# Moving the residual halves of stationary weights by 64 bytes, and what makes room for it, in a single-precision decoder block

## The chip, the cores and the metric

The kernel runs on one core of a Trainium2 chip. The metric is the device time of one execution in microseconds (us); three runs gave a median of 1689.5 us.

## The reference, cut to what matters

One layer of a decoder block on 256 tokens with a model width of 2048, all in single precision:

```python
proj = x @ w_in                              # 2048 -> 13336 columns: q, k, v, gates of both mixers
y_gla = gated_linear_attention(...) @ w_branch_gla
y_fox = forgetting_attention(...) @ w_branch_fox
x = layer_norm(ALPHA * x + (sigmoid(ma) * y_gla + sigmoid(mb) * y_fox) @ w_out)
g = causal_dwconv(x @ w_gate, conv_w, conv_b)          # width 3 over the tokens, 5632 channels
x = layer_norm(ALPHA * x + (gelu(g) * (x @ w_up)) @ w_down)
x = x + sigmoid(x @ w_ple_gate) * (p @ w_ple_proj)
```

Nearly all the work is products of 256 tokens with weight matrices that are each read once.

## The kernel before, in words

**Split products.** A single-precision operand v is split into hi, which is v rounded to the format that TensorE takes at full rate (fp32r), and lo = v - hi. A product of two operands is three of such halves: hi by hi, lo by hi and hi by lo. ScalarE writes hi (`copy`, the activations of L96) and VectorE writes lo (the subtractions, L163 for most of the weights).

**Units.** The weights come in 284 units of 128 x 2048 elements, numbered u in the order of their use. `prep` (L150) takes one unit in two halves, for each of which SyncE loads a `raw` tile of 128 x 1024, ScalarE makes `hi` and VectorE makes `lo`. `unit` (L169) hands the next one out and keeps two more prepared ahead. `prep_s` (L128) with `pair512` (L116) does it for those units of the down projection that go by a seven-product scheme.

**Two ways of using a unit.** TensorE holds one operand, the stationary one, of 128 x 128, and streams the other, the moving one, past it; each product has its own weight load (PEld in the profile), which runs beside the product ahead of it.

- Weights stationary: `w_unit` (L221). For each of 16 slices of the contraction, hi is the stationary operand and streams 512 columns, the tokens' hi and lo side by side (L227). Then lo is stationary and streams the 256 columns of the tokens' hi (L229). The two are called a pair here. The stages, by the names of their results: psfq, psfk, psq, psk (u 0 to 31), psm (u 64 to 95), psa and psb (u 96 to 119), psg and psu (gate and up, u 136 to 223). The first three units of gate and up go through `w_phase` (L233), which streams 256 columns at a time.
- Activations stationary: `x_half` with `x_mm` (L285, L258, products at L271). The tokens' hi or lo is stationary and 512 columns of the weights' hi or lo stream past. The stages are gv and gr (u 32 to 63), wo (u 120 to 135), pg (last 16 units). The down projection dn (L1101, u 224 on) has activations stationary as well.

In psfq to psk, psm, gv and gr small products of the attention are put between the large ones (`pull`); psa, psb, psg and psu have none between them.

**Where the tiles lie.** The pools are laid out one after another. Numbers are bytes within a partition. The six places of hi start at 25,088 and follow each other every 4,096, and those of lo start at 49,664, every 4,096: all are multiples of 512. `gap` (L64) puts unused columns ahead of rhi (96 columns) and behind rlo (192 columns). The work tiles `s8`, which hold activations, lie at 75,008 and every 8,192 after it: each starts 256 bytes past a multiple of 512. So in `w_unit` the moving operand starts 256 past a multiple of 512 and the stationary one at a multiple; in `x_half` it is the other way round.

**First stage.** fv takes 16 half units of 128 x 1048 of its own (`fv_prep`, L338), with activations stationary and three moving chunks of 352, 352 and 344 columns (`fch`, L335; products at L381). The hi and lo tiles are `s8` tiles with their first column at the tile's start. Both halves of the first unit are loaded in three chunks each, the others whole. Two of the five `raw` places are taken at first by `held` tiles, which GpSimd releases by a copy that waits for a lo tile (L361 for the first half of unit 0, L364 for its second half): the loads of later halves, which need these places, wait for that on SyncE's queue.

**Gate.** In the loop over 44 blocks (L1017) the gate's result is combined into `gp`, one of two tiles of 264 columns whose first two columns are zero for good (L991). GpSimd copies two columns behind the data (L1023), and VectorE takes the three taps of the convolution from it (L1025, L1030).

**Work tiles t1 and t2** are rings of six places each, of 256 and 512 columns, for short-lived results.

Of the kernel before, what the change touches and what calls it, by code (L numbers as in the profile page):

```python
# [9 lines left out]
F32 = mybir.dt.float32  # L10
F32R = mybir.dt.float32r
# [8 lines left out]
P = 128  # L20
# [6 lines left out]
FH = 8  # L27
# [5 lines left out]
NS = 1048  # L33


GAPS = (96, 192, 64)
P_STAT = 5000
P_LN1 = (4000, 2000)
P_LN2 = (4000, 1000)
# [17 lines left out]
def tile_block(ctx: ExitStack, tc: tile.TileContext, wu, wfv, wpp, xT_in, x_in, pT_in, wlr,  # L57
               chan, gnorm, lng, ident_in, mask_in, cmask_in, out):
    nc = tc.nc
# [20 lines left out]
    def s8(shape, dt=F32, name=None):  # L80
        return big.tile(shape, dt, tag="S8", name=name)
# [4 lines left out]
    def t2(name):  # L86
        return sm.tile([P, 512], F32, tag="t2", bufs=6, name=name)
# [7 lines left out]
    def copy(o, i, scale=1.0):  # L95
        return nc.scalar.activation(o, i, AF.Copy, bias=0.0, scale=scale)  # L96
# [16 lines left out]
            for i, n in enumerate(DN_ORDER[nh]) if n in DN_S}  # L113
    ready = {}

    def pair512(a, b, name):  # L116

        hi, lo = [r.tile([P, 1024], F32R, tag=t, name=f"{t}{name}")
                  for r, t in ((rhi, "hi"), (rlo, "lo"))]
        out = []  # L120
        for src, e in ((a, slice(0, 512)), (b, slice(512, 1024))):
            if src is not None:
                copy(hi[:, e], src)
                nc.vector.tensor_tensor(lo[:, e], src, hi[:, e].bitcast(F32), ALU.subtract)
                out.append((hi[:, e], lo[:, e]))
        return out

    def prep_s(u):  # L128

        r0, r1 = [ring.tile([P, 1024], F32, tag="raw", bufs=5, name=f"raw{u}_{h}")  # L130
                  for h in range(2)]
        for h, r in enumerate((r0, r1)):
            nc.sync.dma_start(r, wu[u, :, h * 1024:(h + 1) * 1024])
        b12, b11, b22, b21 = r0[:, 0:512], r0[:, 512:1024], r1[:, 0:512], r1[:, 512:1024]
        ops = pair512(b11, None, f"b11_{u}")
        hi = rhi.tile([P, 1024], F32R, tag="hi", name=f"hi{u}_1")
        copy(hi, r1)
        lo = rlo.tile([P, 1024], F32R, tag="lo", name=f"lo{u}_1")
        nc.vector.tensor_tensor(lo, r1, hi.bitcast(F32), ALU.subtract)
        ops += [(hi[:, 512:1024], lo[:, 512:1024]), (hi[:, 0:512], lo[:, 0:512])]  # L140
        ts = {}
        for n, a, b in (("T1", b12, b11), ("T3", b12, b22), ("T2", b22, "T1"),
                        ("T4", b21, "T2")):
            ts[n] = t2(f"{n}_{u}")
            nc.vector.tensor_tensor(ts[n], a, ts.get(b, b) if isinstance(b, str) else b,
                                    ALU.subtract)
        ops += pair512(ts["T1"], ts["T3"], f"t13_{u}") + pair512(ts["T2"], ts["T4"], f"t24_{u}")
        ready[u] = ops

    def prep():  # L150
        u = n_prep[0]
        n_prep[0] += 1
        if u in dn_s:
            prep_s(u)
            return
        his, los = [], []
        for h in range(2):
            raw = ring.tile([P, 1024], F32, tag="raw", bufs=5, name=f"raw{u}_{h}")
            nc.sync.dma_start(raw, wu[u, :, h * 1024:(h + 1) * 1024])
            hi = rhi.tile([P, 1024], F32R, tag="hi", name=f"hi{u}_{h}")  # L160
            copy(hi, raw)
            lo = rlo.tile([P, 1024], F32R, tag="lo", name=f"lo{u}_{h}")
            nc.vector.tensor_tensor(lo, raw, hi.bitcast(F32), ALU.subtract)  # L163
            his.append(hi)
            los.append(lo)
        ready[u] = (his, los)
# [165 lines left out]


    fv = s8([P, 2, 1024], name="fv")
    fch = ((0, 352), (352, 352), (704, 344))  # L335
    fbk = [[mmtile(f"fv_{t}{c}") for c in range(3)] for t in range(2)]

    def fv_prep(u, hs=(0, 1), his=None, los=None):  # L338
        his, los = his or [], los or []
        for h in hs:  # L340
            raw = ring.tile([P, NS], F32, tag="raw", bufs=5, name=f"fvraw{u}_{h}")
            hi = s8([P, NS], F32R, name=f"fvhi{u}_{h}")
            lo = s8([P, NS], F32R, name=f"fvlo{u}_{h}")
            if u > 0:
                nc.sync.dma_start(raw, wfv[u, :, h, :])
            for o, n in fch if u < 2 else ((0, NS),):
                e = slice(o, o + n)
                if u == 0:
                    nc.sync.dma_start(raw[:, e], wfv[u, :, h, e])
                copy(hi[:, e], raw[:, e])  # L350
                nc.vector.tensor_tensor(lo[:, e], raw[:, e], hi[:, e].bitcast(F32), ALU.subtract)
            his.append(hi)
            los.append(lo)
        return his, los
# [3 lines left out]
    held = [ring.tile([P, NS], F32, tag="raw", bufs=5, name=f"held{i}") for i in range(2)]  # L358
    load_x(0, 0, 1, 1)
    f0 = fv_prep(0, (0,))  # L360
    nc.gpsimd.tensor_copy(held[0][:, 0:1], f0[1][0][:, NS - 1:NS].bitcast(F32))  # L361
    load_x(0, 1, 2, 1)
    fvu = [fv_prep(0, (1,), *f0)]
    nc.gpsimd.tensor_copy(held[1][:, 0:1], f0[1][1][:, NS - 1:NS].bitcast(F32))  # L364
    load_x(0, 2, 4)
    fvu.append(fv_prep(1))
    for u in range(8):
        hi, lo = fvu[u]
        for j in range(2):
            kt = 2 * u + j  # L370
            a = xT[kt // 4][:, kt % 4, :]
# [6 lines left out]
            for t, i, c in seq:  # L378
                o, n = fch[c]
# [27 lines left out]
    for t in range(2):  # L407
        tk = t1("smtok")
        nc.gpsimd.memset(tk, 0.0)
        for i in range(3):  # L410
            copy(tk[:, 32 * i:32 * i + 16], fbk[t][2][:, 320:336])
        copy(tk[:, P:P + FH], fbk[t][2][:, 336:344])
        nc.tensor.transpose(smp[:GROWS, t * P:t * P + P], tk[:, 0:GROWS], ident)
        nc.tensor.transpose(smp[:FH, 256 + t * P:256 + t * P + P], tk[:, P:P + FH], ident)
    for t in range(2):
        for c, (o, n) in enumerate(fch):
            n = min(n, 1024 - o)
# [145 lines left out]
    for nm, dst, sc in (("fq", fq, P ** -0.5), ("fk", fk, 1.0)):  # L563
        if nm == "fk":
            mixers.append(fox_gen())
        for n in range(8):
            hi, lo = unit()
# [415 lines left out]


    tc.keep_in_program_order(nc.scalar.preload_act_table_set("gelu_apprx_tanh_and_others"))


    gp = [late.tile([P, 264], F32, name=f"gp{i}") for i in range(2)]
    late.tile([P, GAPS[2]], F32, name="gap2")
    for i in range(2):  # L990
        nc.gpsimd.memset(gp[i][:, 0:2], 0.0)  # L991
    hC, hS, hY, yps = {}, {}, [], {}

    def sums(y, pair):
# [21 lines left out]

    for n in range(NF):  # L1017
        psg = gate_up(f"psg{n}")
        g = gp[n % 2]
        comb(psg, g[:, 2:258])  # L1020
        cw = [chn[:, c_cw + j * NF + n:c_cw + j * NF + n + 1] for j in range(3)]
        for i in range(2):
            nc.gpsimd.tensor_copy(g[:, 258 + i:259 + i], g[:, 129 - i:130 - i])  # L1023
        y = t1("yc")
        nc.vector.tensor_scalar(y, g[:, 2:258], cw[2], chn[:, c_cb + n:c_cb + n + 1],  # L1025
                                ALU.mult, ALU.add)
        y3 = y.rearrange("p (b n) -> p b n", b=2)
        for j, o in ((1, 1), (0, 0)):
            tap = g[:, o:o + 264 - 4 * o].rearrange("p (b n) -> p b n", b=2)[:, :, 0:P]
            nc.vector.scalar_tensor_tensor(y3, tap, cw[j], y3, ALU.mult, ALU.add)  # L1030
        nc.scalar.activation(y, y, AF.Gelu_apprx_tanh, bias=0.0, scale=1.0)
        psu = gate_up(f"psu{n}")
        u = t1("up")
        comb(psu, u)
        pair, j = n // 2, n % 2
        if pair in DN_S:
            if j == 0:
                if pair in DN_Y:
                    if not hY:
                        hY.append(s8([P, len(DN_Y), 2, 256], name="hY"))  # L1040
                    yps[pair] = hY[0][:, DN_Y.index(pair)]
                else:
# [310 lines left out]
```

## Time and profile before

| | |
|---|---|
| three runs | 1688.66, 1689.5, 1692.32 us |
| profiled execution | 1692.31 us, of which the span 1690.2 us |
| TensorE products, weight loads | busy 1679.6 us and 1445.2 us |
| VectorE, ScalarE | busy 1178.1 us and 861.7 us |
| GpSimd | busy 37.4 us |
| granted clock of TensorE | 1.000 |

The span runs from the first to the last instruction; the 2.1 us between it and the execution's own time lie around it. A row of a group of instructions has the line, the engine, the operation, result<-operands with buffer numbers left out, the count, then the busy time in us and the mean ns of one, and last the engine's idle time ahead of them with what ended it. The end of a product in the trace is modelled, and a product's time reaches into that of the next one: start to start is less than the mean of one.

### The profile page before, as it was taken

How to read it: one execution, taken by the hardware profiler on the slowest of the kernel's cores; microseconds unless marked ns; L12 is line 12 of the kernel's file. 1: busy time of each engine (PE TensorE's matmuls, PEld its weight loads, DVE VectorE, ACT ScalarE, POOL GpSimd, SP SyncE). 2: the span in 40 equal slices, each digit the busy share in tenths (PEclk: the TensorE clock that was granted, in tenths of full speed). 3: DMA queues.
4: the chain of work that ended last, by engine and by line, in shares of the span. 5: the costliest groups of instructions: out<-in, count | busy, mean ns of one | idle time of the engine just before them, and what ended most of it. 6: DMA issues, size and time to landing. Idle time of an engine off the chain costs nothing.

```text
span 1690.2 us, 23985 instructions
## 1 busy us (share of the span) xinstructions
PE 1679.6 (99%) x8986; PEld 1445.2 (86%) x8986; DVE 1178.1 (70%) x1762; ACT 861.7 (51%) x1267; POOL 37.4 (2%) x125
## 2 busy tenths in 40 slices
PE   9999999999999999999999999999999999999998
PEld 8888888888888888888888888888888888887887
DVE  7656658768756547774687777766666798788764
ACT  6645445445555544444364444444444465455543
POOL 0100000000000000000010000000000000000000
PEclk9999999999999999999999999999999999999999
DMA  8755555555555555557655665555555556677544
GB/s 318 254 178 164 169 180 182 176 183 177 177 174 173 162 188 193 191 188 290 215 175 188 211 212 187 187 187 186 186 185 189 188 173 209 205 257 245 177 167 169
DMA packets 91717, 330.24 MB, mean 195 GB/s; under 512 B 10264, under 2 KB 11936, under 8 KB 90448
## 3 DMA queue, kind: packets, MB, share of 16 engines
q1 hardware_dynamic: 90816, 324.51, 57.8%
q0 software_dynamic: 784, 4.20, 0.7%
q8 instruction: 70, 1.15, 0.3%
q14 instruction: 47, 0.39, 0.1%
HBM read 323.42 MB, written 5.25 MB: 194 GB/s over the span
## 4 chain that ended last, share of the span: by engine, by line
PE 89%; DVE 5%; DMA 4%; issue 1%; ACT 0%; SPq 0%; POOL 0%; DVEq 0%; ACTq 0%
PE psu L227 10%; PE psg L227 9%; PE psm L227 7%; PE gr L271 5%; PE gv L271 5%; PE psu L229 5%; PE wo L271 5%; PE pg L271 5%; PE dn L1101 5%; PE psg L229 5%; PE psm L229 4%; PE psa L227 3%; DMA raw<-in_wu_dram 3%; PE fv L381 2%; PE psa L229 2%; PE psk L227 2%
## 5 line engine op out<-in xcount | busy, mean ns | idle before, releaser
L163 DVE TENSOR_TENSOR lo<-raw,hi 128x1024 fp32r<-128x1024 f32 x536 | 653.9, 1223 | 392.0 <-ACT hi L96 391.3
L96 ACT ACTIVATE hi<-raw 128x1024 fp32r<-128x1024 f32 x552 | 583.8, 1060 | 656.0 <-issue 263.9
L227 PE MATMUL psu<-x1T,hi 128*128 128x512 f32 x688 | 245.0, 399 | 0.0
L227 PE MATMUL psg<-x1T,hi 128*128 128x512 f32 x672 | 239.3, 399 | 0.0
L229 PE MATMUL psu<-x1T,lo 128*128 128x256 f32 x688 | 193.2, 281 | 0.0
L229 PE MATMUL psg<-x1T,lo 128*128 128x256 f32 x672 | 188.7, 281 | 0.0
L227 PE MATMUL psm<-xT,hi 128*128 128x512 f32 x512 | 180.1, 395 | 0.0
L227 PEld LDWEIGHTS psu<-x1T,hi 128*128 128x128 f32 x688 | 129.3, 188 | 32.2
L227 PEld LDWEIGHTS psg<-x1T,hi 128*128 128x128 f32 x672 | 126.3, 188 | 31.5
L229 PE MATMUL psm<-xT,lo 128*128 128x256 f32 x512 | 143.4, 280 | 0.0
L229 PEld LDWEIGHTS psu<-x1T,lo 128*128 128x128 f32 x688 | 130.0, 189 | 0.0
L229 PEld LDWEIGHTS psg<-x1T,lo 128*128 128x128 f32 x672 | 127.0, 189 | 0.0
L1101 PE MATMUL dn<-hi,hC 128*128 128x512 f32 x448 | 124.0, 389 | 1.2 <-ACT hi L96 1.2
L227 PEld LDWEIGHTS psm<-xT,hi 128*128 128x128 f32 x512 | 96.0, 187 | 21.8
L1101 PEld LDWEIGHTS dn<-hi,hC 128*128 128x128 f32 x448 | 84.0, 188 | 19.0 <-ACT hi L96 1.6
L229 PEld LDWEIGHTS psm<-xT,lo 128*128 128x128 f32 x512 | 96.7, 189 | 0.2
L227 PE MATMUL psa<-oT,hi 128*128 128x512 f32 x256 | 89.5, 391 | 0.0
L271 PE MATMUL gv<-hi,xT 128*128 128x512 f32 x256 | 72.3, 394 | 0.0
L271 PE MATMUL gr<-hi,xT 128*128 128x512 f32 x256 | 72.2, 394 | 0.0
L229 PE MATMUL psa<-oT,lo 128*128 128x256 f32 x256 | 71.7, 280 | 0.0
L1101 PE MATMUL dn<-lo,hC 128*128 128x512 f32 x224 | 70.6, 390 | 0.7 <-DVE lo L163 0.7
L271 PE MATMUL wo<-hi,mT 128*128 128x512 f32 x256 | 70.2, 390 | 0.0
(285 smaller groups left out, 2768.6 us busy)
## 6 DMA issues: line engine op xcount, KB each, us to landing
raw<-in_wu_dram SPq DMA_DIRECT2D x568, 512.0 KB, 4.0
fvraw<-in_wfv_dram SPq DMA_DIRECT2D x14, 524.0 KB, 6.7
lnb<-in_lng_dram SPq DMA_DIRECT2D x4, 1024.0 KB, 9.6
z<-in_x_dram SPq DMA_DIRECT2D x2, 1024.0 KB, 7.6
praw<-in_wpp_dram SPq DMA_DIRECT2D x4, 512.0 KB, 5.8
x1d<-z POOLq DMA_DIRECT2D x2, 1024.0 KB, 5.9
z<-x1d SPq DMA_DIRECT2D x4, 512.0 KB, 5.8
xraw<-in_xT_dram SPq DMA_DIRECT2D x7, 256.0 KB, 6.8
```

The source lines that it names most:

```text
L96: return nc.scalar.activation(o, i, AF.Copy, bias=0.0, scale=scale)
L163: nc.vector.tensor_tensor(lo, raw, hi.bitcast(F32), ALU.subtract)
L227: nc.tensor.matmul(ps, lhsT=hi[i // 8 if hoff == 0 else 0][:, w0 % 1024:w0 % 1024 + P], rhs=a[:, kt % 4, :], start=first and i == 0, stop= ...
L229: nc.tensor.matmul(ps[:, 256:512], lhsT=lo[i // 8 if hoff == 0 else 0][:, w0 % 1024:w0 % 1024 + P], rhs=a[:, kt % 4, 0:256], start=False, ...
L271: nc.tensor.matmul(bs[j][:, 0:m], lhsT=x, rhs=v[:, o:o + m], start=first and i == 0, stop=last and i == 2)
L381: nc.tensor.matmul(fbk[t][c][:, 0:n], lhsT=x, rhs=w[:, o:o + n], start=kt == 0 and i == 0, stop=kt == 15 and i == 2)
L1101: nc.tensor.matmul(ps, lhsT=x, rhs=w, start=todo[id(ps)] == total[id(ps)], stop=todo[id(ps)] == 1)
```

## The change

Three parts.

**Lo tiles.** The places of lo grow from 1024 to 1152 columns (4,608 bytes, still a multiple of 512). The new `lo_tile` gives back 1024 columns of such a place, from column 16 on (64 bytes) for units whose weights are stationary, and from column 0 for units whose activations are (u 32 to 63, 120 to 135, 224 to 283). hi stays where it was. The gap behind rlo shrinks from 192 to 64 columns, so that the work tiles still start 256 bytes past a multiple of 512.

**Gate.** The two `gp` tiles go. Each block takes a `t2` tile instead, and GpSimd writes its two zero columns anew each time, 44 times in all.

**First stage.** The chunks are 384, 384 and 280 columns. The hi and lo tiles of fv begin 64 columns (256 bytes) into their places, so that each chunk starts at a multiple of 512 bytes. Only the first half of unit 0 is loaded in chunks. The copy that releases the first `held` tile waits for the lo of the second half of unit 0, and the one for the second waits for the lo of the first half of unit 1.

```diff
-GAPS = (96, 192, 64)
+GAPS = (96, 64, 80)
+LO_SHIFT = 16
+UA = (range(32, 64), range(120, 136), range(224, 284))
...
+    def lo_tile(u, name):
+        o = 0 if any(u in r for r in UA) else LO_SHIFT
+        return rlo.tile([P, 1152], F32R, tag="lo", name=f"lo{name}")[:, o:o + 1024]
...
-            lo = rlo.tile([P, 1024], F32R, tag="lo", name=f"lo{u}_{h}")
+            lo = lo_tile(u, f"{u}_{h}")
             nc.vector.tensor_tensor(lo, raw, hi.bitcast(F32), ALU.subtract)
...
-    fch = ((0, 352), (352, 352), (704, 344))
+    fch = ((0, 384), (384, 384), (768, 280))
...
-            hi = s8([P, NS], F32R, name=f"fvhi{u}_{h}")
-            lo = s8([P, NS], F32R, name=f"fvlo{u}_{h}")
-            if u > 0:
+            hi = s8([P, 64 + NS], F32R, name=f"fvhi{u}_{h}")[:, 64:]
+            lo = s8([P, 64 + NS], F32R, name=f"fvlo{u}_{h}")[:, 64:]
+            chunked = u + h == 0
+            if not chunked:
                 nc.sync.dma_start(raw, wfv[u, :, h, :])
...
     f0 = fv_prep(0, (0,))
-    nc.gpsimd.tensor_copy(held[0][:, 0:1], f0[1][0][:, NS - 1:NS].bitcast(F32))
     load_x(0, 1, 2, 1)
     fvu = [fv_prep(0, (1,), *f0)]
-    nc.gpsimd.tensor_copy(held[1][:, 0:1], f0[1][1][:, NS - 1:NS].bitcast(F32))
+    nc.gpsimd.tensor_copy(held[0][:, 0:1], f0[1][1][:, NS - 1:NS].bitcast(F32))
     load_x(0, 2, 4)
-    fvu.append(fv_prep(1))
+    f1 = fv_prep(1, (0,))
+    nc.gpsimd.tensor_copy(held[1][:, 0:1], f1[1][0][:, NS - 1:NS].bitcast(F32))
+    fvu.append(fv_prep(1, (1,), *f1))
...
-    gp = [late.tile([P, 264], F32, name=f"gp{i}") for i in range(2)]
     late.tile([P, GAPS[2]], F32, name="gap2")
-    for i in range(2):
-        nc.gpsimd.memset(gp[i][:, 0:2], 0.0)
...
     for n in range(NF):
         psg = gate_up(f"psg{n}")
-        g = gp[n % 2]
+        g = t2(f"gp{n}")
+        nc.gpsimd.memset(g[:, 0:2], 0.0)
         comb(psg, g[:, 2:258])
```

The order of the large products on TensorE is the same in both programs. The following shows where other queues differ. First, SyncE's queue at the start of the program before (x is the activations, fvraw the halves of the first stage's weights):

```order
L183 DMA xraw<-in_xT_dram 128x256
L349 DMA fvraw_0_136<-in_wfv_dram 128x352 x2
L349 DMA fvraw_0_136<-in_wfv_dram 128x344
L183 DMA xraw<-in_xT_dram 128x256
L349 DMA fvraw_1_153<-in_wfv_dram 128x352 x2
L349 DMA fvraw_1_153<-in_wfv_dram 128x344
L183 DMA xraw<-in_xT_dram 128x512
L345 DMA fvraw_0_170<-in_wfv_dram 128x1048
L345 DMA fvraw_1_180<-in_wfv_dram 128x1048
L345 DMA fvraw_0_226<-in_wfv_dram 128x1048
```

And the same queue after the change:

```order
L191 DMA xraw<-in_xT_dram 128x256
L359 DMA fvraw_0_136<-in_wfv_dram 128x384 x2
L359 DMA fvraw_0_136<-in_wfv_dram 128x280
L191 DMA xraw<-in_xT_dram 128x256
L355 DMA fvraw_1_152<-in_wfv_dram 128x1048
L191 DMA xraw<-in_xT_dram 128x512
L355 DMA fvraw_0_167<-in_wfv_dram 128x1048
L355 DMA fvraw_1_178<-in_wfv_dram 128x1048
L355 DMA fvraw_0_224<-in_wfv_dram 128x1048
```

The second half of unit 0 has become one load; the order is otherwise the same, and the last two rows wait for the `held` places, one half unit later than before. Second, GpSimd's queue in the gate loop before the change, where the x1d transfer writes a layer norm's result out:

```order
L1023 COPY gp_8163<-gp_8163 128x1 x2
L1023 COPY gp_8164<-gp_8164 128x1 x2
L982 DMA x1d<-z_7211 128x2048
L1023 COPY gp_8163<-gp_8163 128x1 x2
L1023 COPY gp_8164<-gp_8164 128x1 x2
```

And after it:

```order
L1028 MEMSET gp_8738 128x2
L1028 MEMSET gp_8850 128x2
L1028 MEMSET gp_8960 128x2
L1032 COPY gp_8518<-gp_8518 128x1 x2
L1032 COPY gp_8628<-gp_8628 128x1 x2
L993 DMA x1d<-z_7209 128x2048
L1032 COPY gp_8738<-gp_8738 128x1 x2
L1032 COPY gp_8850<-gp_8850 128x1 x2
```

The zeroing of a block's tile stands several blocks ahead of its copies, and x1d has kept its place between the copies of the sixth and the seventh block.

More of the change, by code (lines that the diff above doesn't have):

```diff
@@ L114, in tile_block, with pair512 @@
     ready = {}
-    def pair512(a, b, name):
-        hi, lo = [r.tile([P, 1024], F32R, tag=t, name=f"{t}{name}")
-                  for r, t in ((rhi, "hi"), (rlo, "lo"))]
+    def lo_tile(u, name):
+        o = 0 if any(u in r for r in UA) else LO_SHIFT
+        return rlo.tile([P, 1152], F32R, tag="lo", name=f"lo{name}")[:, o:o + 1024]
+    def pair512(u, a, b, name):
+        hi = rhi.tile([P, 1024], F32R, tag="hi", name=f"hi{name}")
+        lo = lo_tile(u, name)
         out = []
@@ L134, in prep_s @@
         b12, b11, b22, b21 = r0[:, 0:512], r0[:, 512:1024], r1[:, 0:512], r1[:, 512:1024]
-        ops = pair512(b11, None, f"b11_{u}")
+        ops = pair512(u, b11, None, f"b11_{u}")
         hi = rhi.tile([P, 1024], F32R, tag="hi", name=f"hi{u}_1")
         copy(hi, r1)
-        lo = rlo.tile([P, 1024], F32R, tag="lo", name=f"lo{u}_1")
+        lo = lo_tile(u, f"{u}_1")
         nc.vector.tensor_tensor(lo, r1, hi.bitcast(F32), ALU.subtract)
@@ L146, in prep_s @@
                                     ALU.subtract)
-        ops += pair512(ts["T1"], ts["T3"], f"t13_{u}") + pair512(ts["T2"], ts["T4"], f"t24_{u}")
+        ops += pair512(u, ts["T1"], ts["T3"], f"t13_{u}") + pair512(u, ts["T2"], ts["T4"], f"t24_{u}")
         ready[u] = ops
@@ L347, in fv_prep @@
                 e = slice(o, o + n)
-                if u == 0:
+                if chunked:
                     nc.sync.dma_start(raw[:, e], wfv[u, :, h, e])
@@ L410, in tile_block @@
         for i in range(3):
-            copy(tk[:, 32 * i:32 * i + 16], fbk[t][2][:, 320:336])
-        copy(tk[:, P:P + FH], fbk[t][2][:, 336:344])
+            copy(tk[:, 32 * i:32 * i + 16], fbk[t][2][:, 256:272])
+        copy(tk[:, P:P + FH], fbk[t][2][:, 272:280])
         nc.tensor.transpose(smp[:GROWS, t * P:t * P + P], tk[:, 0:GROWS], ident)
```

## The prediction

> **What bounds the kernel now.** I read the page first. Its parts on busy time and on the chain say that TensorE is never out of work:
>
> ```profile
> PE 1679.6 (99%) x8986; PEld 1445.2 (86%) x8986; DVE 1178.1 (70%) x1762; ACT 861.7 (51%) x1267; POOL 37.4 (2%) x125
> PE 89%; DVE 5%; DMA 4%; issue 1%; ACT 0%; SPq 0%; POOL 0%; DVEq 0%; ACTq 0%
> ```
>
> Next the view of waits, for TensorE alone, its longest first:
>
> ```profile
> PE fv L381 <- ACT fvhi L96: 1.4, 1, 1.4
> PE warm_ps L106 <- DVE warm L103: 1.2, 1, 1.2
> PE dn L1101 <- ACT hi L96: 1.2, 1, 1.2
> ```
>
> No wait is worth more than 1.4 us. So the change can save much only by making the products follow each other faster, and the question is whether they do so at one rate. The view of windows counts the products in two stretches of 100 us in which nothing but pairs of L227 and L229 runs, psa and psb first, then psg and psu. Its columns are the stretch, its length, busy time (count) of TensorE, weight loads, VectorE, ScalarE and GpSimd, then the clock, the DMA share and GB/s:
>
> ```profile
> 660.00:760.00 100.00, 100.00 (x579) 88.19 (x578) 71.62 (x109) 48.34 (x72) 0.00 (x0) 1.00 0.59 190
> 1000.00:1100.00 100.00, 100.00 (x568) 86.77 (x567) 70.64 (x108) 50.07 (x74) 3.35 (x18) 1.00 0.58 186
> ```
>
> The same instructions, at the same clock and with TensorE busy throughout: 200 / 579 = 0.3454 us for a pair in the first, 200 / 568 = 0.3521 in the second. The difference is 6.7 ns a pair. The timeline shows it product by product, first in psb, then in psu (start and duration in us):
>
> ```profile
> 699.84 0.39 PE L227 MATMUL psb<-ofT,hi 128*128 128x512 f32 x1
> 700.19 0.39 PE L227 MATMUL psb<-ofT,hi 128*128 128x512 f32 x1
> 700.53 0.39 PE L227 MATMUL psb<-ofT,hi 128*128 128x512 f32 x1
> 700.88 0.39 PE L227 MATMUL psb<-ofT,hi 128*128 128x512 f32 x1
> ```
>
> ```profile
> 899.84 0.40 PE L227 MATMUL psu<-x1T,hi 128*128 128x512 f32 x1
> 900.08 0.28 PE L229 MATMUL psu<-x1T,lo 128*128 128x256 f32 x1
> 900.20 0.40 PE L227 MATMUL psu<-x1T,hi 128*128 128x512 f32 x1
> 900.43 0.28 PE L229 MATMUL psu<-x1T,lo 128*128 128x256 f32 x1
> 900.55 0.40 PE L227 MATMUL psu<-x1T,hi 128*128 128x512 f32 x1
> 900.78 0.28 PE L229 MATMUL psu<-x1T,lo 128*128 128x256 f32 x1
> 900.90 0.40 PE L227 MATMUL psu<-x1T,hi 128*128 128x512 f32 x1
> ```
>
> Three pairs take 1.04 us above and 1.06 us below. Below, the hi products are 0.24, 0.23 and 0.23 us ahead of the next start and the lo products 0.12 each. The groups of the page and of the view by line tell which stages are slow: the mean of a hi product is 391 ns in the fast rhythm and 399 in the slow one.
>
> ```profile
> L227 PE MATMUL psu<-x1T,hi 128*128 128x512 f32 x688 | 245.0, 399 | 0.0
> L227 PE MATMUL psg<-x1T,hi 128*128 128x512 f32 x672 | 239.3, 399 | 0.0
> L229 PE MATMUL psu<-x1T,lo 128*128 128x256 f32 x688 | 193.2, 281 | 0.0
> L227 PE MATMUL psm<-xT,hi 128*128 128x512 f32 x512 | 180.1, 395 | 0.0
> L227 PE MATMUL psa<-oT,hi 128*128 128x512 f32 x256 | 89.5, 391 | 0.0
> L229 PE MATMUL psa<-oT,lo 128*128 128x256 f32 x256 | 71.7, 280 | 0.0
> L227 PE MATMUL psfk<-xT,hi 128*128 128x512 f32 x128 | 46.0, 403 | 0.0
> L227 PE MATMUL psfq<-xT,hi 128*128 128x512 f32 x128 | 45.4, 397 | 0.0
> L227 PE MATMUL psb<-ofT,hi 128*128 128x512 f32 x128 | 45.1, 391 | 0.0
> ```
>
> The loss lies with the hi product (8 ns in its mean) and hardly with the lo product (281 against 280). While a hi product streams, the weights of the next lo product are loaded; that load is the one whose address the change moves. This is my reason to expect an effect, and there is one against it: in the last third of psm the same places give the fast rhythm, as the view by line of 594 to 627 us shows, while psm as a whole has 395.
>
> ```profile
> L227 PE MATMUL psm<-xT,hi 128*128 128x512 f32 x96 | 33.3, 391 | 0.0
> ```
>
> So the address alone does not set the rhythm; how a stage is entered does too. The old placement allows both rhythms, and whether the new one allows the slow one is what no row of before can show.
>
> **The change part by part.** *Lo tiles.* If the slow rhythm goes: psu and psg have 688 + 672 = 1360 pairs, all slow, at 6.7 ns: 9.1 us. psm has 512 pairs at a mean halfway between 391 and 399, so half of them slow: 256 x 6.7 ns = 1.7 us. The first 32 units (psfq, psfk, psq, psk) have 512 pairs; their means, 397 to 403, also hold other waits of single products, so I cannot read the share that is slow and take half as in psm, 1.7 us, with bounds of 0 and 512 x 6.7 ns = 3.4. psa and psb stay. Sum: 12.5 us, all on the path, since TensorE is busy throughout. For the stages with activations stationary, and for hi, nothing moves against multiples of 512 bytes, and the chain gives one steady rate there (24 products in 5.46 us, 0.2275 each, time after time):
>
> ```profile
> 257.99 5.46 PE gv L271 x24
> 263.89 5.46 PE gv L271 x24
> ```
>
> They count for nothing. VectorE writes the shifted tile with the same instruction, which is no part of the sum either.
>
> *First stage.* The columns and the number of products stay; only the arrivals move. The timeline has ScalarE taking what has landed and the product that needs it, and the chain has the load that TensorE's 1.4 us wait hangs on:
>
> ```profile
> 6.64 0.94 ACT L96 ACTIVATE fvhi<-fvraw 128x352 fp32r<-128x352 f32 x2 [0.35 <-DMA fvraw<-in_wfv_dram]
> 7.21 0.89 PE L381 MATMUL fv<-fvhi,xT 128*128 128x352 f32 x4
> 8.06 0.49 ACT L96 ACTIVATE fvhi<-fvraw 128x344 fp32r<-128x344 f32 x1 [0.48 <-DMA fvraw<-in_wfv_dram]
> 4.96 6.22 DMA fvraw<-in_wfv_dram
> 11.76 40.13 PE fv L381 x252
> ```
>
> The load issued at 4.96 lands at 11.18, and TensorE, which starts again at 11.76 after 1.4 us, has been out of work since about 10.3. One load in place of three in front of it should save some of the queue's time (three issues become one), so the whole 1.4 us is the most there is to gain. Against it, the first columns of the second half now come only with its last, near 8 us in place of 6.6, and TensorE takes them at 7.2: about 1.3 us with the copy, at most. The later release of the held places delays the loads of the second half of unit 1 and the first of unit 2; queued behind these on SyncE are the next activations, for which TensorE would wait. I take -0.4, with bounds of -1.4 and +1.5.
>
> *Gate.* The zeroing is 44 instructions on GpSimd, which waits 452.1 us for the gate in any case:
>
> ```profile
> POOL gp L1023 <- DVE gp L254: 452.1, 44, 13.0
> 0.74 0.10 POOL L202 MEMSET mhalf<- 128x1 f32 x1 [0.29 <-POOLq L1340]
> L1030 DVE SCALAR_TENSOR_TENSOR yc<-gp,chn,yc 128x256 f32<-128x256 f32 x88 | 42.6, 484 | 8.0
> ```
>
> At 0.10 us each that is 4.4 us of cover of 452.1: nothing. What is new is that the zeroing waits for a t2 place, with the copies of earlier blocks behind it in GpSimd's queue, and VectorE's taps behind those, and the next lo tiles behind the taps. The order has the zeroing several blocks ahead and each t2 place is given up within a block or two, so I take 0. If the cover were gone, the 8.0 us that VectorE already loses ahead of the taps would grow; until TensorE feels that, VectorE's idle 30% must be used up. Bounds 0 and +1.5 us.
>
> The sum is -12.5 - 0.4 = -12.9 us: a span of 1677.3, an execution of 1692.3 - 12.9 = 1679.4. The profiled execution is 2.8 us above the median, so for the median of runs I write 1689.5 - 12.9 = 1676.6, about **1677 us**. By itself this case runs from 1674 (early stages fully slow, the first stage at its best: -15.6) to 1683 (only psg and psu mend, first stage and gate at their worst: -9.1 + 3.0).
>
> **The rivals.** *The address does not matter.* TensorE enters gate and up in the same order as before and falls into the same slow rhythm, since the fast and the slow rhythm were both found at the old places. For it speaks the quoted stretch of psm; against it that the loss is on the hi product alone. The lo part of the sum is 0 and the time 1689.5, between 1688 and 1692. If the entry happens to change, psg and psu come out fast by chance: 1689.5 - 9.1 = 1680.4. The Trainium skill has a rule that speaks for this and against the change: "TensorE: Matmul & The Clock Gate", in the section on what each phase of a matmul is for, says that the array reads moving and stationary operands through two independent ports, so that loading the next weights takes no bandwidth from the running product. By that rule the two windows above should not differ; they do, by 6.7 ns a pair, though it stays open whether the two reads are the reason.
>
> *The shift breaks the fast rhythm.* Then every pair runs at 0.3521 us. What is fast now is 256 + 128 pairs of psa and psb, 256 of psm and as many of the early stages: 896 x 6.7 ns = 6.0 us, so 1695.5. It decides as soon as psa and psb lose their 579 products in 100 us. For it speaks that the present offset of 256 bytes between moving and stationary operand is the only one at which I have seen the fast rhythm of pairs; against it that the stretch with the slow one has the same offset.
>
> *The gain is a step larger.* A pair might fall below 0.3454 us. One more step of the same size on all 2768 pairs would be another 18.5 us: 1677 - 18.5 = 1658. Nothing in the profile shows such a pair. The same page of the Trainium skill, in its section on the back-to-back issue gap, gives N / 2.4 + 2.5 ns, which for 512 and 256 columns is an estimate of 325 ns a pair and would leave 2768 x 20 ns = 55 us below the fast rhythm; the fastest stretch here, at a granted clock of 1.00, has 345, so the trace does not bear it out for products that each load weights.
>
> **How the numbers follow.** Forecast 0.55; no effect 0.20, of which 0.05 with a lucky entry; fast rhythm broken 0.17; larger gain 0.08. Of this kernel a measurement can tell about 0.2%, 3.4 us, from no change. Faster by more: 0.55 + 0.05 + 0.08 = 0.68. Same: 0.15. Slower: 0.17. The range reaches from 1672, a little below the forecast's own end, to 1695.5, the price of the broken rhythm; it leaves out the larger gain (0.08) and the dearer half of the broken rhythm (some 0.09).
>
> **What would show it.** Right: some 579 products in each 100 us of gate and up, the means of psu and psg hi at 391 in place of 399, that of psm too, psa and psb and the stages at L271 unchanged, fv's wait below 1.4 us. Wrong in the main step: psu and psg at 399 again, or psa at 399. Wrong in the gate: a wait of TensorE on lo in gate and up, with GpSimd late. Wrong in the first stage: a wait of fv on its activations near 17 us.

## The result, and the profile after

| | before | after |
|---|---|---|
| median of 6 runs each | 1689.64 us | 1678.68 us |
| lowest to highest | 1688.66 to 1692.32 | 1677.58 to 1679.77 |
| profiled execution, its span | 1692.31, 1690.2 | 1678.59, 1676.8 |

The ratio is 0.9933, with a 95% interval of 0.9921 to 0.9946; it is estimated from all the runs, while the two medians alone would give 0.9935. The forecast was 1677 us.

The page of the kernel after, its part on busy time:

```profile
PE 1668.2 (99%) x8986; PEld 1447.4 (86%) x8986; DVE 1177.3 (70%) x1762; ACT 862.3 (51%) x1267; POOL 43.1 (3%) x167
```

TensorE runs the same 8986 products and is as fully busy as before, for 11.4 us less. The view of windows, again one stretch in psa and psb and one in psg and psu (the first 10 us earlier than in the view of before, since the stage now ends earlier):

```profile
650.00:750.00 100.00, 100.00 (x579) 88.41 (x578) 71.49 (x108) 48.48 (x73) 0.00 (x0) 1.00 0.56 190
1000.00:1100.00 100.00, 100.00 (x579) 88.44 (x578) 71.76 (x110) 50.62 (x75) 4.78 (x32) 1.00 0.57 190
```

Gate and up now have 579 products in 100 us, where they had 568; psa and psb keep theirs. The timeline in the middle of gate and up (start and duration in us) shows the pairs:

```profile
899.48 0.39 PE L235 MATMUL psu<-x1T,hi 128*128 128x512 f32 x1
899.70 0.28 PE L237 MATMUL psu<-x1T,lo 128*128 128x256 f32 x1
899.82 0.39 PE L235 MATMUL psu<-x1T,hi 128*128 128x512 f32 x1
900.05 0.28 PE L237 MATMUL psu<-x1T,lo 128*128 128x256 f32 x1
900.17 0.39 PE L235 MATMUL psg<-x1T,hi 128*128 128x512 f32 x1
900.40 0.28 PE L237 MATMUL psg<-x1T,lo 128*128 128x256 f32 x1
900.51 0.39 PE L235 MATMUL psg<-x1T,hi 128*128 128x512 f32 x1
```

Three pairs now take 1.03 us, from 899.48 to 900.51. The groups of the view by line, for the rows that the prediction gave of before:

```profile
L235 PE MATMUL psu<-x1T,hi 128*128 128x512 f32 x688 | 240.5, 392 | 0.0
L235 PE MATMUL psg<-x1T,hi 128*128 128x512 f32 x672 | 234.9, 392 | 0.0
L237 PE MATMUL psu<-x1T,lo 128*128 128x256 f32 x688 | 192.3, 280 | 0.0
L235 PE MATMUL psm<-xT,hi 128*128 128x512 f32 x512 | 178.9, 393 | 0.0
L235 PE MATMUL psa<-oT,hi 128*128 128x512 f32 x256 | 89.5, 392 | 0.0
L1110 PE MATMUL dn<-lo,hC 128*128 128x512 f32 x224 | 70.5, 390 | 0.6 <-DVE lo L171 0.6
L279 PE MATMUL wo<-hi,mT 128*128 128x512 f32 x256 | 70.2, 389 | 0.0
L235 PE MATMUL psq<-xT,hi 128*128 128x512 f32 x128 | 45.9, 401 | 0.0
L235 PE MATMUL psfk<-xT,hi 128*128 128x512 f32 x128 | 45.6, 399 | 0.0
```

The hi products of psu and psg have gone from 399 to 392 ns, the lo products are where they were (281 to 280). The view of waits, TensorE alone, has nothing over 1.2 us. Its row of fv is another wait than the one of before, as is said under the first stage below:

```profile
PE warm_ps L110 <- DVE warm L107: 1.2, 1, 1.2
PE ptl L829 <- issue: 0.7, 1, 0.7
PE dn L1110 <- DVE lo L171: 0.6, 1, 0.6
PE fv L392 <- ACT fvhi L100: 0.5, 1, 0.5
```

**By stage.** The means of such rows contain overlaps. A sharper number is the time from the start of one product to the start of the next (a step), averaged over a stage from the starts in the trace; for a pair the steps of hi and lo are added, and products that waited are left out of the mean. The last column adds up the steps of all the stage's own products, waits included; the small products put between them are not in it.

| stage | pair before, ns | pair after, ns | stage, us |
|---|---|---|---|
| psu and psg (1360 pairs) | 353.33 | 346.67 | 480.5 to 471.5 |
| psm (512) | 349.13 | 346.76 | 179.5 to 178.4 |
| psfq, psfk, psq, psk (512) | 350.11, 349.87, 347.84, 353.46 | 346.84, 346.79, 346.94, 346.89 | 182.1 to 180.4 |
| psa (256) | 346.63 | 346.62 | no change |
| psb (128) | 346.73 | 346.75 | no change |
| dn | | | 231.4 to 229.7 |
| fv | | | 47.6 to 47.4 |

wo and pg stayed within 0.1 us. A pair of the slow rhythm has its hi product 236.5 ns ahead of the next start and its lo product 116.8; a pair after the change 229.6 and 117.1. So the loss was between the start of a hi product and the start of the lo product behind it. The loads themselves do not show it: the weight loads of psu have a mean of 188 ns for hi in both kernels, and of 189 for lo before and 190 after.

**By stretch.** A mean over a stage can hide more than one rhythm. In the trace of before, the pairs fall into 37 stretches of a dozen pairs or more with no other product between them. Each stretch keeps one rhythm throughout: 22 of them are at 346.6 to 346.7 ns and 15 at 352.6 to 353.4. In psm it is 6 stretches of 12 that are slow, 192 of the 512 pairs. The 13th begins in psm and runs on through psa and psb without a break, 512 pairs at 346.7; and gate and up are a single stretch, which is slow. In the trace of after, all 37 stretches are at 346.6 to 346.9 ns.

### The profile page after: what moved, and what is told of

Same layout as the page of the kernel before. It is cut to its first block, busy times and chain, and to the rows that moved or that the text cites. A ratio compares the mean times of both kernels' runs of the same rounds, so it can differ in the third digit from the quotient of the medians.

```text
span 1676.8 us, 23988 instructions
## 1 busy us (share of the span) xinstructions
PE 1668.2 (99%) x8986; PEld 1447.4 (86%) x8986; DVE 1177.3 (70%) x1762; ACT 862.3 (51%) x1267; POOL 43.1 (3%) x167
## 4 chain that ended last, share of the span: by engine, by line
PE 83%; DVE 8%; DMA 6%; issue 2%; ACT 1%; SPq 0%; POOL 0%; DVEq 0%; ACTq 0%
PE psg L235 9%; PE psu L235 9%; PE psm L235 7%; PE gr L279 5%; PE gv L279 5%; PE wo L279 5%; PE pg L279 5%; PE psu L237 5%; DMA raw<-in_wu_dram 5%; PE psg L237 5%; PE psm L237 4%; PE psa L235 4%; DVE lo L171 2%; PE dn L1110 2%; PE psa L237 2%; PE psfq L235 2%
## 5 line engine op out<-in xcount | busy, mean ns | idle before, releaser
L235 PE MATMUL psu<-x1T,hi 128*128 128x512 f32 x688 | 240.5, 392 | 0.0
L235 PE MATMUL psg<-x1T,hi 128*128 128x512 f32 x672 | 234.9, 392 | 0.0
```

What stands on the lines that cost most here:

```text
L235: nc.tensor.matmul(ps, lhsT=hi[i // 8 if hoff == 0 else 0][:, w0 % 1024:w0 % 1024 + P], rhs=a[:, kt % 4, :], start=first and i == 0, stop= ...
```

## The experiments

Each edit is one to the kernel after the change, each ratio one to the kernel before, timed on the same chip. "The pair" is the start-to-start mean just described; the columns of a windows row are those of the prediction's.

**The shift taken back, the rest kept.** Gate and first stage stay as changed, and lo lies at 0 everywhere.

```diff
-LO_SHIFT = 16
+LO_SHIFT = 0
```

> The changed kernel with lo back at column 0 of its wider place; gate and first stage stay as changed. If the 64 bytes mend the rhythm: psu and psg are slow again (568 products in 100 us, mean of hi 399 ns) and the time is about 1678.7 + 9.1 + 1.1 to 2.8 = 1689 to 1691 us. If the other edits changed how the stages are entered: psu and psg stay fast (579, 391 ns) and the time stays within 2 us of 1678.7.

Measured: 1689.56 us, ratio 1.0001 (0.9992 to 1.0010). Every stage has the pairs of before within 0.1 ns, but for psfq (349.3 against 350.1), and gate and up run at 568 products again:

```profile
650.00:750.00 100.00, 100.00 (x579) 88.17 (x578) 71.46 (x108) 48.46 (x74) 0.00 (x0) 1.00 0.56 190
1000.00:1100.00 100.00, 100.00 (x568) 86.72 (x567) 70.64 (x108) 49.93 (x74) 4.71 (x32) 1.00 0.56 187
```

The whole gain is the 64 bytes. Gate and first stage together are worth nothing that can be measured (within 1.7 us). Stretch by stretch, too, slow and fast are where they were before, the first one of psfq excepted.

**The shift at 256 bytes.**

```diff
-LO_SHIFT = 16
+LO_SHIFT = 64
```

> lo 64 columns (256 bytes) into its place in place of 16, so that it starts where the moving activations start when counted from a multiple of 512. If any distance from hi's address class mends the rhythm: as with 64 bytes, about 1679 us. If what counts is the distance between lo and the operand that streams while it loads, this is the extreme case (distance 0) and pairs run slow or slower: 1690 us or more.

Measured: 1689.16 us, ratio 0.9999 (0.9989 to 1.0009), with the slow rhythm in gate and up:

```profile
1000.00:1100.00 100.00, 100.00 (x568) 86.72 (x567) 70.50 (x108) 50.10 (x74) 4.72 (x32) 1.00 0.56 187
```

The streaming operand starts 256 bytes past a multiple of 512, so here lo and the streaming operand start at the same place within 512 bytes, and at 0 they do not. It makes no difference: 256 acts as 0, and slow and fast lie in the same stretches as with lo at 0. So the rhythm that an entry brings repeats, for the most part, from one execution to the next.

**The shift at 128 bytes.**

```diff
-LO_SHIFT = 16
+LO_SHIFT = 32
```

> lo 32 columns (128 bytes) into its place. If any shift mends the rhythm: about 1679 us, 579 products in 100 us of gate and up. If 64 bytes is a narrow choice: between 1679 and 1690 us, with a rhythm of its own.

Measured: 1681.45 us, ratio 0.9954 (0.9939 to 0.9969), from four runs of two sorts, 1679.55 and 1679.59, 1684.02 and 1683.31. The profiled one was the 1679.55. In it gate and up are fast (346.7 ns, 579 products), psfq to psk are not (348.5 to 350.0), and psm is between (347.6). So at 128 bytes more than one rhythm is possible still. The other two are some 4 us longer; 1360 pairs of gate and up at the 350.0 ns that psfq to psk reach here would make 4.5 us, but that is an estimate, and no such run was profiled.

**64 bytes where activations are stationary too.**

```diff
-UA = (range(32, 64), range(120, 136), range(224, 284))
+UA = ()
```

> lo 64 bytes into its place for all units, also where activations are stationary and lo is the moving operand. If the address of the moving operand matters in the same way as that of the stationary one: gv, gr, wo, dn or pg become slower than 24 products in 5.46 us; a tenth of the 6.7 ns on their 2500 products would be 1.7 us, all of it 17 us. If only the loads of weights matter: within 1 us of 1678.7 us.

Measured: 1685.91 us, ratio 0.9981 (0.9971 to 0.9990): 7.2 us more than with the change as it is. The stages with activations stationary carry it, with psu as it was:

```profile
L235 PE MATMUL psu<-x1T,hi 128*128 128x512 f32 x688 | 240.4, 392 | 0.0
L1110 PE MATMUL dn<-lo,hC 128*128 128x512 f32 x224 | 72.1, 397 | 0.0
L279 PE MATMUL wo<-hi,mT 128*128 128x512 f32 x256 | 71.4, 394 | 0.0
```

The row of wo is that of its hi products, whose own place has not moved: they go from 389 to 394 ns, beside products on lo that go from 389 to 393, so the loss does not fall on the moved operand's products alone. dn's products on lo go from 390 to 397; by stage, dn takes 232.7 us, wo 89.2 against 87.4, gv 89.7 against 88.5, gr 89.9 against 88.8. The same 64 bytes that help a stationary lo harm a streaming one, and the exceptions in `UA` are worth more than half of what the shift brings.

**hi and lo both at 64 bytes.** The gap ahead of hi grows by 64 bytes, which moves both rings, and the gap behind lo shrinks by as much, so that the work tiles stay.

```diff
-GAPS = (96, 64, 80)
+GAPS = (112, 48, 80)
-LO_SHIFT = 16
-UA = (range(32, 64), range(120, 136), range(224, 284))
+LO_SHIFT = 0
+UA = ()
```

> hi and lo both 64 bytes past a multiple of 512, in all units; the activations stay 256 past one. If the distance between lo and the operand that streams while lo loads is what counts: psu and psg fast (579 products in 100 us) as with lo alone. If the distance between hi and lo counts: they are again equal, so psu and psg slow (568). In both cases the stages with activations stationary have hi and lo as moving operands at 64 and lose at least what lo alone at 64 lost there (7 us).

Measured: 1700.2 us, ratio 1.0061 (1.0038 to 1.0084). psa, fast in every other kernel so far, is slow as well:

```profile
650.00:750.00 100.00, 100.00 (x568) 86.91 (x567) 69.99 (x106) 47.80 (x72) 0.00 (x0) 1.00 0.56 187
1000.00:1100.00 100.00, 100.00 (x568) 86.86 (x567) 70.12 (x107) 50.06 (x74) 4.20 (x29) 1.00 0.56 187
```

The pairs are at 352.7 to 353.3 ns in every stage. So lo's place against the streaming operand, which is here as after the change, does not decide by itself.

**hi at 64 bytes, lo at 0.** The same gaps, with lo moved on by 448 bytes to the next multiple of 512.

```diff
-GAPS = (96, 64, 80)
+GAPS = (112, 48, 80)
-LO_SHIFT = 16
-UA = (range(32, 64), range(120, 136), range(224, 284))
+LO_SHIFT = 112
+UA = ()
```

> hi 64 bytes past a multiple of 512 and lo at a multiple, in all units. If the distance between lo and the operand that streams while lo loads counts: psu and psg can be slow (568 in 100 us) as with both at 0, unless hi's own load matters too. If the distance between hi and lo counts: fast (579).

Measured: 1699.1 us, ratio 1.0044 (1.0029 to 1.0059); two of the six runs were near 1694.6, and the profiled one was not one of them. In it gate and up have 353.33 ns a pair, psa 350.0, psm 347.6:

```profile
650.00:750.00 100.00, 100.00 (x574) 87.92 (x573) 71.07 (x107) 47.58 (x72) 0.00 (x0) 1.00 0.55 189
1000.00:1100.00 100.00, 100.00 (x569) 86.97 (x567) 71.16 (x109) 49.60 (x74) 4.71 (x32) 1.00 0.56 188
```

With hi at 64 no place of lo tried so far gives the fast rhythm in gate and up of the profiled executions. There the split of a pair has moved: the step of lo, from its start to the next hi, is 118.3 ns with both at 64 and 119.6 here, where it is 117.1 after the change. The load of the next hi starts in that step.

But hi at 64 does not cost everywhere. The 347.6 ns of psm are a mean of two rhythms: four of its stretches, 120 pairs in all, are at 340.0 ns and the others at 350.0. The first of the four, and the stretch behind it:

```profile
498.00:507.00 9.00, 9.00 (x55) 7.98 (x54) 4.90 (x9) 5.17 (x9) 1.12 (x2) 1.00 0.41 139
511.00:520.00 9.00, 9.00 (x53) 7.90 (x52) 6.11 (x8) 4.69 (x7) 0.00 (x0) 1.00 0.53 180
```

340.0 ns are 226.8 for hi and 113.3 for lo, one more step of 6.67 ns below the fast rhythm, and 226.8 is no more than the 512 columns of wo or dn take with activations stationary. No other profiled kernel has a stretch in this rhythm, and whether these places could bring it to whole stages was not tried. As for the question of the experiment, lo lies 64 bytes behind hi here and 64 ahead after the change, so the distance between the two is not tested yet.

**hi at 64 bytes, lo at 128.** The same distance from hi to lo as after the change, both 64 bytes further on.

```diff
-GAPS = (96, 64, 80)
+GAPS = (112, 48, 80)
-UA = (range(32, 64), range(120, 136), range(224, 284))
+UA = ()
```

> hi starts 64 bytes past a multiple of 256 and lo 128 past it, in every stage; the work tiles stay. So lo is 64 bytes ahead of hi, as after the change, but both stand 64 further against the streaming operand. If the distance from hi to lo alone sets the rhythm, every weight-stationary pair is at 346.7 ns (579 products in 100 us of gate and up), and the time is 1686 us plus 1 to 3 us for hi at 64 where it streams. If hi's own place against the streaming operand matters too, pairs are slower: 347.6 to 353.3 ns as with hi at 64 and lo at 0 or 64, 568 to 575 products, and 1693 to 1700 us. I expect the second, with a chance of two in three.

Measured: 1701.44 us, ratio 1.0058 (1.0042 to 1.0075). psu and psg have 353.33 ns a pair, psa 350.00, psm 350.3:

```profile
650.00:750.00 100.00, 100.00 (x574) 88.02 (x573) 71.24 (x108) 47.55 (x72) 0.00 (x0) 1.00 0.57 188
1000.00:1100.00 100.00, 100.00 (x568) 87.56 (x567) 70.22 (x106) 49.44 (x73) 4.21 (x29) 1.00 0.57 188
```

The distance from hi to lo does not set the rhythm alone. In gate and up the step of hi is 231.7 ns, 2.1 more than after the change, and that of lo 121.7, 4.6 more: most of the loss has gone over to the step in which the load of the next hi starts. All three kernels with hi at 64 lose in that step of gate and up, whatever the place of lo. The time is above the range expected. Against the profiled execution of after, the pairs cost 13.9 us and the stages with activations stationary 9.7, dn at 233.3 us and wo at 89.2 among them; with lo alone at 64 everywhere the latter lost 7.8.

**The rhythm disturbed, at 0.** Six transposes of the identity, whose results nothing reads, stand between blocks of gate and up and make TensorE enter the rest anew; lo lies at 0.

```diff
+        if n in (8, 14, 20, 26, 32, 38):
+            pd = mxtile(f"between{n}")
+            nc.tensor.transpose(pd[:, 0:P], ident, ident)
         psg = gate_up(f"psg{n}")
-LO_SHIFT = 16
+LO_SHIFT = 0
```

> lo at column 0 as in the first experiment, and six single transposes put between the units of gate and up, one every sixth block, with results that nothing reads. If the entry decides between two rhythms that the placement at 0 allows: some of the stretches between two transposes run fast (346 to 347 ns a pair) and some slow (353), and the time lies between 1680 and 1690 us. If the placement alone decides: all of them slow, 1690 us.

Measured: 1686.46 us, ratio 0.9981 (0.9969 to 0.9992). One window of 50 us in each of the last six of the seven stretches that the transposes make:

```profile
955.00:1005.00 50.00, 50.00 (x285) 43.39 (x284) 37.18 (x57) 24.58 (x37) 2.85 (x16) 1.00 0.63 209
1020.00:1070.00 50.00, 50.00 (x291) 44.16 (x290) 35.34 (x54) 25.32 (x38) 2.28 (x12) 1.00 0.56 190
1090.00:1140.00 50.00, 50.00 (x285) 43.42 (x284) 33.91 (x48) 23.25 (x34) 2.63 (x15) 1.00 0.56 188
1155.00:1205.00 50.00, 50.00 (x291) 44.15 (x290) 33.87 (x48) 24.18 (x35) 2.53 (x14) 1.00 0.56 190
1225.00:1275.00 50.00, 50.00 (x290) 44.11 (x290) 34.00 (x49) 24.23 (x34) 2.64 (x15) 1.00 0.56 188
1290.00:1340.00 50.00, 50.00 (x285) 43.40 (x284) 32.98 (x48) 23.81 (x33) 2.15 (x10) 1.00 0.55 182
```

285 products are the slow rhythm, 290 or 291 the fast one. The pairs of all seven stretches are at 353.3, 353.4, 346.7, 353.4, 346.7, 346.7 and 353.4 ns: at the same places counted from multiples of 512 bytes, with the same instructions, each entry falls into one of two rhythms and holds it for some 190 pairs, to the next disturbance. What in an entry chooses the rhythm is not shown. Three stretches of 191 pairs are fast, at 6.67 ns a pair 3.8 us, less the time of the transposes; the median is 3.0 us below before's on that chip (1689.47).

**The rhythm disturbed, at 64.** The same six transposes in the kernel after the change.

```diff
+        if n in (8, 14, 20, 26, 32, 38):
+            pd = mxtile(f"between{n}")
+            nc.tensor.transpose(pd[:, 0:P], ident, ident)
         psg = gate_up(f"psg{n}")
```

> The changed kernel with the same six transposes. If the 64 bytes leave only the fast rhythm: every stretch between two transposes is fast and the time is the changed kernel's plus about 6 x 0.2 us, 1679 to 1681 us. If the changed kernel is fast because of how its stages happen to be entered: some stretches are slow and the time is up to 1688 us.

Measured: 1678.53 us, ratio 0.9932 (0.9910 to 0.9955). The first and the last of the same six stretches:

```profile
955.00:1005.00 50.00, 50.00 (x290) 44.24 (x289) 36.94 (x57) 25.02 (x37) 2.39 (x13) 1.00 0.63 211
...
1285.00:1335.00 50.00, 50.00 (x290) 44.21 (x290) 36.08 (x53) 23.97 (x34) 2.15 (x10) 1.00 0.56 188
```

All seven stretches are at 346.7 ns, and so are the 36 of the stages ahead of gate and up, within 0.1 ns. At 64 bytes none of the entries seen, 37 in the kernel after and 43 here, falls into the slow rhythm, where 15 of 37 did before: the shift does not bring a lucky entry, it takes the slow rhythm away.

**192 and 448 bytes.** Two kernels, with the place of lo at 192 past a multiple of 512 and, 256 further, at 448.

```diff
-LO_SHIFT = 16
+LO_SHIFT = 48
```

> lo 192 bytes into its place where weights are stationary, hi at a multiple of 512. 0 and 256 bytes gave the same times, product by product, so the addresses may count by their place within 256 bytes. The theory that any placement of lo off hi's own class mends the pairs expects 1679 to 1681 us here; the theory that the direction of the shift counts expects something between 1681 and 1700 us.

```diff
-LO_SHIFT = 16
+LO_SHIFT = 112
```

> lo 448 bytes into its place, which is 192 + 256. If addresses count by their place within 256 bytes, pairs have the same rhythm as at 192 in every stage (the count of products in 100 us within 1, the time within 2 us). If they count within 512 bytes or more, the two differ.

Measured: 1685.87 us, ratio 0.9979 (0.9969 to 0.9988), and 1685.49 us, ratio 0.9976 (0.9966 to 0.9986). psu and psg are at 351.11 ns in both, a third rhythm; psa is at 346.68. No stage's pair differs by more than 0.05 ns between the two. The row of gate and up at 192:

```profile
1000.00:1100.00 100.00, 100.00 (x571) 87.29 (x571) 71.01 (x109) 49.86 (x73) 4.73 (x32) 1.00 0.56 186
```

As with 0 and 256, the place within 256 bytes is what counts in these two pairs of kernels, and a shift in the other direction by 64 (192 is 256 - 64) is not the same as one by 64.

**The old first stage.** Chunks, bases, loads and `held` copies of the first stage as before; lo tiles and gate as changed. The reads of the last chunk's result move back with its columns (256 to 320 and 272 to 336).

```diff
-    fch = ((0, 384), (384, 384), (768, 280))
+    fch = ((0, 352), (352, 352), (704, 344))
...
-            hi = s8([P, 64 + NS], F32R, name=f"fvhi{u}_{h}")[:, 64:]
-            lo = s8([P, 64 + NS], F32R, name=f"fvlo{u}_{h}")[:, 64:]
-            chunked = u + h == 0
+            hi = s8([P, NS], F32R, name=f"fvhi{u}_{h}")
+            lo = s8([P, NS], F32R, name=f"fvlo{u}_{h}")
+            chunked = u == 0
```

> The changed kernel with the first stage of before (chunks of 352, 352 and 344, tiles at the start of their places, both halves of unit 0 in chunks, the held places released as before). By the prediction the new first stage is worth 0.4 us, between -1.5 and +1.4: so 1679 us, with TensorE's wait in fv back at 1.4 us. If the first stage has a larger part in the gain: 1681 us or more.

Measured: 1677.55 us, ratio 0.9931 (0.9911 to 0.9950), by intervals no other than the change. TensorE's wait in fv, which the old first stage was to have at 1.4 us:

```profile
PE fv L391 <- ACT fvhi L100: 0.4, 1, 0.4
```

The wait in fv with the new first stage and lo at 128 bytes:

```profile
PE fv L392 <- ACT fvhi L100: 1.5, 1, 1.5
```

The two rows look alike and are different waits: the first ends at 11.65 us, ahead of the third half unit, the second at 8.85, ahead of the second. Each varies from one profiled execution to the next, 0.4 and 1.4 us with the old first stage, none to 1.5 with the new one. This kernel is also the lowest of all by its median, but not by its interval; no version was found that can be told to be better than the change.

## Why the prediction was right

**The bound.** TensorE's products stand end to end and the gain could only come from their rhythm: shown. Busy time of TensorE fell by 11.4 us, the span by 13.4, and the kernel with lo back at 0 loses all of it.

**psu and psg, 9.1 us forecast.** 1360 pairs by 6.67 ns are 9.07 us; the stage lost 9.0. The forecast's 6.7 ns, worked out from two counts of 579 and 568, was the pair's own step.

**psm, 1.7 us.** Mis-sized: 1.1 us. Half of the pairs were taken as slow, by a mean halfway between 391 and 399. Its pairs stood at 349.13 ns, which is (349.13 - 346.67) / 6.67 = 37% of the way. They are the 192 pairs of the six slow stretches. The mean of 395 held other waits too, as the 393 that remains shows; it is not the 391 that was to be seen.

**psfq to psk, 1.7 us.** Right at 1.7, though the guess of one half hid shares of 18% in psq and all in psk. Their means still stand at 394 to 401 ns with all pairs fast: as the prediction said of 397 to 403, these rows cannot be read for the rhythm, since single products there wait for something else.

**psa, psb and the stages with activations stationary, 0.** Right for the change as it is. For psa and psb that rests on luck: before, they were part of one unbroken stretch whose entry happened to be fast, and the same places made gate and up slow. For the stages with activations stationary it rests on lo at 0 for those units; the kernel with lo at 64 everywhere shows that this is worth 7.2 us.

**First stage, -0.4 us.** Both halves of the reasoning are in the trace, and they cancel. The 1.4 us wait, ahead of the product at 11.76 of before, is gone: TensorE comes to that half unit at 11.80 and does not wait. In its place stands the wait that was feared on the second half of unit 0. Its first columns are copied at 8.25 us in place of 6.64, and the product on them starts at 8.83 in place of 7.21. From the timeline of after:

```profile
8.25 1.26 ACT L100 ACTIVATE fvhi<-fvraw 128x384 fp32r<-128x384 f32 x3 [1.45 <-DMA fvraw<-in_wfv_dram]
8.83 0.96 PE L392 MATMUL fv<-fvhi,xT 128*128 128x384 f32 x4 [0.46 <-ACT fvhi L100]
11.80 0.86 PE L392 MATMUL fv<-fvhi,xT 128*128 128x384 f32 x4
```

So the 0.5 us in the view of waits is not what is left of the 1.4, and the sign "fv's wait below 1.4 us" came true for another wait. The wait is short here because the first four products took 1.84 us and TensorE came late to it; with lo at 128 bytes they took 0.97, the wait was 1.48, and TensorE was at 11.81 all the same. The stage as a whole went from 47.6 to 47.4 us and lies between 46.9 and 47.9 in the other profiled executions, and the medians with the old and the new first stage are 1.1 us apart the other way, inside the interval: within its bounds of -1.4 and +1.5 the effect cannot be told from 0. The wait near 17 us is not in the view of waits.

**Gate, 0.** Right. The zeroing is 44 instructions, and GpSimd does wait for its places, but TensorE knows nothing of it. GpSimd's groups in the kernel after:

```profile
L1032 POOL COPY gp<-gp 128x1 f32<-128x1 f32 x88 | 20.8, 270 | 391.2 <-DVE gp L262 380.6 <-DMA raw<-in_wu_dram 10.7
L1028 POOL MEMSET gp<- 128x2 f32 x44 | 3.7, 99 | 46.4 <-DVE yc L1039 25.2 <-DVE hS L1012 14.0 <-PE psg L237 7.2
```

3.7 us of work and 46.4 us of waits for a t2 place, out of a cover that was 452.1 us and is still 380.6. VectorE's idle time ahead of the taps went from 8.0 to 8.4 us.

**The sum.** Pairs: 9.0 + 1.1 + 1.7 = 11.8 us where the forecast had 12.5. Span against span the change is 13.4 us: 11.8, 0.2 in fv and 1.7 in dn, 13.7, less some tenths lost elsewhere. The 1.7 was not predicted and is not the change's: the long waits of dn add up to 2.7 us in the profiled execution of before, to 1.1 in that of after, and to 0, 1.6, 0.8 and 0 with lo at 0, 256, 128 and 64 everywhere. That execution of before was 2.7 us above its median. Median against median the change is 11.0 us, beside 11.8 for the pairs.

**The rivals.** That the address does not matter is refuted, by the kernels with lo at 0, 192 and 448. The half of it that speaks of the entry is true: at 0 the entry decides. It is at 64 that no entry seen has a say, which the prediction could not know from rows of before. The rule of the Trainium skill quoted there ("TensorE: Matmul & The Clock Gate", on what each phase of a matmul is for), of two independent read ports and a load that takes no bandwidth from the running product, would have left the time at 1689.5; the same products with lo 64 bytes on give 1678.68, and with hi there as well 1700.2 (1701.44 with lo moved on by as much). The runs show that the place of the weights decides which paces a pair can fall into; that two reads meet in the memory is a guess, which no run here shows, since the loads keep their 187 to 190 ns.

The broken rhythm came true to its price in another place: all pairs slow was forecast at 1695.5, 6.0 us more than before, and with hi and lo together at 64 the pairs do cost 5.9 us more; the rest of the 1700.2 lies in the stages with activations stationary (dn 230.7 us, wo 88.2). The change escapes it because hi stays. The larger gain did not show in the change: no stage of any kernel has a mean pair under 346.6 ns. But the rhythm that it needs exists: the four stretches of psm at 340.0 ns, with hi at 64 and lo at 0, are just the one more step of 6.7 ns that the prediction priced at 18.5 us.

## What to carry to other kernels

When TensorE is busy throughout, count identical instructions in equal windows of different stages, and take starts rather than durations: two rates of the same instructions are a reserve that no wait shows. Look inside a stage as well: the 347.6 ns of psm with hi at 64 and lo at 0 were 340.0 and 350.0. Try the place of each operand within 256 bytes, one operand and one stage at a time, since what helps a stationary tile can harm a streaming one (here 11.0 us against 7.2). Disturb the rhythm on purpose before trusting a good placement, for a lucky entry looks the same until something else in the kernel moves.

## What was not expected of the hardware

- Pairs fall into separate rhythms at the same places, 346.7 and 353.3 ns with lo at 0, and hold one for hundreds of pairs: all 1360 of gate and up in the kernel before. The slow one there repeats every three pairs, with starts 241 + 120, 236 + 113 and 233 + 117 ns apart. Other places have rhythms at 340.0, 350.0 and 351.1 ns.
- Places count within 256 bytes, for a stationary lo with hi at 0, as far as tried: at 0 and 256 the fast and the slow rhythm, at 64 the fast one alone, at 128 from 346.7 to 350.0 ns, at 192 and 448 from 346.7 to 351.1 (stage means). Why 64 and not 192 stays open.
- With hi at 64 and lo at 0, four stretches of psm run at 340.0 ns a pair, faster than any stretch of the change. Why these four stays open.
- A streaming lo at 64 costs up to 7 ns in the mean of a product of 512 columns (dn, 390 to 397).
